# Rotary sums on VectorE instead of GpSimd, and an opening with the root ahead of the first high part and three more unread products

## The chip, the cores and the metric

The kernel runs on one core of a Trainium2 chip. That core has five engines with instruction streams of their own: TensorE (PE, matrix products into PSUM), VectorE (DVE), ScalarE (ACT), GpSimd (POOL) and SyncE (SP, which here only issues transfers). They meet through semaphores. What counts is the device time of one execution in microseconds, the median of several.

## The reference

The reference is a small decoder trunk in float32: 512 positions, width 1024, two layers. Layer 0 mixes positions by retention, layer 1 by an mLSTM; behind each stands a convolutional feed-forward block. Each block is normed by the root mean square, scaled and shifted by values computed from a conditioning vector `c`, and added to the residual. What matters here is the start of it, the retention layer's queries and keys, which get a rotary embedding:

```
def rope(t, positions):
    d = t.shape[-1]
    inv_freq = ROPE_BASE ** (-jnp.arange(0, d, 2, dtype=jnp.float32) / d)
    ang = positions.astype(jnp.float32)[..., None] * inv_freq
    cos = jnp.cos(ang)[:, :, None, :].astype(t.dtype)
    sin = jnp.sin(ang)[:, :, None, :].astype(t.dtype)
    t1, t2 = t[..., : d // 2], t[..., d // 2:]
    return jnp.concatenate([t1 * cos - t2 * sin, t1 * sin + t2 * cos], axis=-1)

def retention_mixer(h, positions, w_in, gn_g, w_out):
    ...
    proj = h @ w_in
    q, k, v, g = jnp.split(proj, [H * dk, 2 * H * dk, 2 * H * dk + H * dv], axis=-1)
    q = rope(q.reshape(Bt, S, H, dk), positions)
    k = rope(k.reshape(Bt, S, H, dk), positions) * (dk ** -0.5)
    ...
        s = jnp.einsum('bhid,bhjd->bhij', qc, kc) * decay
        intra = jnp.einsum('bhij,bhjv->bhiv', s, vc)
```

There are four heads with queries and keys of 256 and values of 512.

## The kernel before

**Products in parts.** Each float32 operand is split into a high part (`hh`, `whi`, `qkh`: a cast on ScalarE) and a low part (`hl`, `wlo`, `qkl`: what the cast left over), and a product is three matmuls: high by high, high by low, low by high. A weight's low part comes either from VectorE (`wlo<-wv,whi`) or in two steps: ScalarE writes the negated high part and a transfer issued by GpSimd adds the weight to it in memory (`wlo<-ws`, `wlo<-wa`, `wlo<-wt`). Some matrix products are formed with fewer blocks from sums of weights, so VectorE also makes sums of weight tiles (`ws<-wv,wv`, `wt<-wa,wb`). ScalarE copies one finished product to `fs`, and VectorE adds it to another (`p<-p,fs`, `pv<-pv,fs`).

**What sets the order.** Nothing is issued as it is written. Every call goes into a `Plan` (class at L153) with a modelled cost; a list scheduler (`order` L222, `run` L268) gives each engine one fixed order by due times counted from TensorE's own order, and only then are the instructions issued, nearly all of them from one line (L387). Moving one step from an engine to another therefore changes the order of its neighbours too. Once the program runs, each engine works through its own fixed list, and an instruction that waits holds up all behind it on that engine. The model charges a VectorE operation more when it runs beside a GpSimd operation with two inputs (`SHARE`, L346 to L350).

**Rotary embedding.** `rope` (L1552) takes the two halves of one head's q or k, each 128 rows by 512 positions, out of PSUM, and forms four products with `cos` and `sin` on VectorE (`rp<-p,cos`; for the first head `rp<-pp,cos`). A difference and a sum of two of these, on GpSimd, give the embedded halves (`rp<-rp,rp`), whose high parts ScalarE casts (`qkh`) and whose low parts VectorE takes (`qkl`). That is done for q and k of four heads: 16 such sums. Heads follow one another, with products of other parts in between; the sums fall between 89 and 315 us.

**The opening.** `ret_start` (L1611) reads x and sums the squares (`pms`, `means`), takes the root on ScalarE (`rc<-pms,eps_t`, L1706) and its reciprocal on VectorE, spreads it over 128 rows by four products with a unit matrix (`pms<-eye,rc`, L1714), scales x with it (`xr`, VectorE), casts (`hh`, ScalarE) and starts the products with the first weights `w_s`, whose high parts are casts (`whi<-raw`, by `high`). While TensorE has nothing to do it is given matmuls of ones whose result is never read (`pst<-warm,ones`, function `busy`, L1623). How many is set by `BUSY` and `EXTRA` (L54 and L55): `BUSY[1] + EXTRA[1]` ahead of the four products with the unit matrix (L1713), `BUSY[2] + EXTRA[2]` behind them (L1717). Those of `EXTRA` have no cost in the plan (`free`). The opening's calls carry one pin, which keeps them in the order in which they are written on each engine.

**Conditioning.** `ada<-ada,c_ext` is a VectorE operation that multiplies a 128x1025 tile of conditioning weights by `c` and sums each row; many of these are spread through the program.

Of the kernel before, what the change touches and what calls it, by code (L numbers as in the profile page):

```python
# [13 lines left out]
AF = mybir.ActivationFunctionType  # L14
ALU = mybir.AluOpType
# [36 lines left out]
HURRY = 1.5  # L52
ROPE_DUE = 200.0
BUSY = (6, 1, 1)  # L54
EXTRA = (4, 1, 3)  # L55
ALIVE = (0, 0, 256, 256, 256, 256, 0, 0)
SUMMED = 6
LOWK = 5
# [332 lines left out]
def trunk(ctx: ExitStack, tc: tile.TileContext, xT, cb, pos, vec, ident, decay, zmask, ada, w_s0, w_in0, w_v0,  # L391
# [20 lines left out]
    def slot(s, dt=F32, w=T):  # L412
        return tile_of(slots, [P, w], dt, "s", uid(s))
# [4 lines left out]
    def bank(s):  # L418
        return tile_of(psum, [P, T], F32, "ps", uid(s))
# [4 lines left out]
    def fixed(pool, shape, dt, name):  # L424
        b = tile_of(pool, shape, dt, name, name)
        b.get()
        return b

    plan = Plan()
    V, A, G, PE, S = (plan.engine(*p) for p in (("DVE", nc.vector), ("ACT", nc.scalar), ("POOL", nc.gpsimd),  # L430
                                                ("PE", nc.tensor), ("SP", nc.sync)))
# [28 lines left out]
    def col(name, i):  # L460
        return vecs[:, VEC[name] + i : VEC[name] + i + 1]

    eps_t = fixed(const, [P, 1], F32, "eps_t")
# [7 lines left out]
    def gemv(layer, f, raw):  # L471
        return V.scalar_tensor_tensor(raw, raw, 1.0, c_ext[:], op0=ALU.mult, op1=ALU.mult,
                                      accum_out=mods[layer][:, f : f + 1])
# [11 lines left out]
    def gain(layer, which, k):  # L485
        f = (8, 32)[which] + k
        i = which * KT + k
        V.tensor_scalar(gains[layer][:, i : i + 1], mods[layer][:, f : f + 1], 1.0,
                        col(("ntok", "nffn")[which], layer * KT + k), op0=ALU.add, op1=ALU.mult)


    def high_part(raw, off=0):
        hi = wide("whi", F32R)[:, off : off + raw.width]
        A.copy(hi, raw)
        return hi
# [158 lines left out]
    def pair_of(s, src):  # L654
        p = Pair(s)
        p.split(src)
        return p
# [894 lines left out]
    def rope(p1, p2):  # L1552
        t = [slot("rp")[:] for _ in range(4)]
        V.tensor_tensor(t[0], p1[:], cos[:], op=ALU.mult)
        V.tensor_tensor(t[1], p2[:], sin[:], op=ALU.mult)
        V.tensor_tensor(t[2], p1[:], sin[:], op=ALU.mult)
        V.tensor_tensor(t[3], p2[:], cos[:], op=ALU.mult)
        G.tensor_tensor(t[0], t[0], t[1], op=ALU.subtract)
        G.tensor_tensor(t[2], t[2], t[3], op=ALU.add)
        return [pair_of("qk", t[n]) for n in (0, 2)]  # L1560

    def half_pair(st, name, finish):
# [48 lines left out]
    def ret_start():  # L1611

        rs, rc = slot("rs"), slot("rc")
        warm = slot("warm", F32R)
        G.memset(warm[:].bitcast(F32), 1.0)
        pss, ps = [bank("pst") for _ in range(5)], bank("pms")
# [6 lines left out]
        def busy(n, w=T, free=0):  # L1623

            for i in range(n):
                c = PE.matmul(pss[0][:, :w], ones["1"][:], warm[:, :w], start=True, stop=True, skip_group_check=True)
                if i >= n - free:
                    c.occ = 0.0
# [9 lines left out]
        def high(k):  # L1638
            wh[k] = high_part(raw[k])
# [11 lines left out]
        def means(m, first):  # L1651

            for t in range(4):
                PE.matmul(ps[:, t : t + 1], sq[m][:, t * P : t * P + P], ones["d"][:, :1].bitcast(F32),
                          start=first and t == 0, stop=True, skip_group_check=True)
# [38 lines left out]
        for m in range(1, KT):  # L1694
# [3 lines left out]
            else:  # L1698
                busy(EXTRA[0], free=EXTRA[0])
                means(m - 1, True)  # L1700
            alive(m, ALIVE[m])
        means(KT - 1, False)
        gemv(0, KT, mod[KT])
        gain(0, 0, 0)
        high(0)
        A.activation(rc[:, :4], ps[:, :4], AF.Sqrt, bias=eps_t[:])  # L1706
        V.reciprocal(rc[:, :4], rc[:, :4])
        pin, plan.pin, plan.soon, plan.behind = plan.pin, None, ROPE_DUE, len(plan.calls) - 1
        for _ in tables:
# [2 lines left out]
        gemv(0, 0, mod[0])  # L1712
        busy(BUSY[1] + EXTRA[1], free=EXTRA[1])  # L1713
        for t in range(4):  # L1714
            PE.matmul(ps[:, t * P : t * P + P], rc[:, t : t + 1].broadcast_to([P, P]), eye[:, :P], start=True,
                      stop=True, skip_group_check=True)
        busy(BUSY[2] + EXTRA[2], free=EXTRA[2])  # L1717
        xr = xrs[0] = slot("xr")
# [45 lines left out]
    def ret_q(i, between=nothing):  # L1764
        thens = [half_pair(R[i], name, rope) for name in ("q", "k")]
        if i:
            fold_pairs(pair_srcs(w_in0, i * 8), sums0.terms, thens, between, i == 2)
            return
        for n, then in enumerate(thens):
            for j in range(2):  # L1770
                proj_item(w_in0[i * 8 + 2 * n + j], h0, then, 2 * n + j in QLOW)
        item([], lambda w: sums_early())
# [167 lines left out]


    sums0.xr.update(ret_start())
    for n, (uses, fn, free) in enumerate(items):
        gate = len(plan.calls)
# [128 lines left out]
```

## Time and profile before

| | |
|---|---|
| median of 3 runs | 1476.16 us (1475.42 to 1477.04) |
| the profiled execution's own time | 1476.27 us |
| its span | 1474.5 us |
| VectorE, of the span | 88% |
| ScalarE | 72% |
| GpSimd | 18% |
| clock granted to TensorE, mean | 0.996 |

The span runs from the first to the last recorded instruction; the execution's time is 1.8 us longer. Times in the rows of the profile count from the start of the span. In a row of the timeline stand the start, the duration, the engine and the line, the operation with the names of what it writes and reads (`out<-in`), its size, and in brackets how long the engine had stood idle before it and which instruction or transfer ended that. In a row of stretches stand the stretch, its length, the busy time of TensorE, its weight loads, VectorE, ScalarE and GpSimd with their instruction counts, the clock granted to TensorE, the share of the transfer engines and their GB/s. In a row of waits stand the total, how often, and the longest.

### The profile page before, as it was taken

To read this page: it belongs to the slowest core of one execution; us is meant where nothing else is said; L and a number is where in the kernel's file an instruction comes from. 1 tells how busy PE (TensorE), PEld (TensorE's weight loads), DVE (VectorE), ACT (ScalarE), POOL (GpSimd) and SP (SyncE) were. 2 spreads that over 40 slices of the span, in tenths; PEclk is the share of its full clock that TensorE was granted. 3 is DMA by queue.
4 is the path that set the end of the run, shared out by engine and by line. 5 is a ranking of instruction groups with operands and counts; after the bars stand their busy time and mean duration, and the time that the engine had idled before them with its cause. 6 is when DMAs were issued, how large, how long until landed. Compare 5 with 4: busy or idle time off the path is not lost. (4 is left out here: it accounts for less than half of the span.)

```text
span 1474.5 us, 27411 instructions
## 1 busy us (share of the span) xinstructions
PE 1457.1 (99%) x10561; PEld 1367.3 (93%) x10561; DVE 1291.8 (88%) x2167; ACT 1064.2 (72%) x1604; POOL 267.9 (18%) x295
## 2 busy tenths in 40 slices
PE   9999999999999999999999999999999999999998
PEld 6899999998999999999999998999989999999997
DVE  7999989787989999898897999999989988886866
ACT  5678858776588776676678985989856877667673
POOL 0334223222011111011001321222121011101010
PEclk9999999999999999999999999999999999999999
DMA  9878989887588999899467876878877678668661
GB/s 365 250 179 202 287 218 245 225 250 197 159 223 216 260 262 256 217 241 246 150 185 171 210 207 188 193 194 198 253 192 191 166 184 204 153 171 205 171 162 59
DMA packets 90822, 306.16 MB, mean 208 GB/s; under 512 B 11954, under 2 KB 14514, under 8 KB 90691
## 3 DMA queue, kind: packets, MB, share of 16 engines
q1 hardware_dynamic: 60882, 197.18, 38.8%
q0 software_dynamic: 29520, 106.97, 38.8%
q8 instruction: 82, 1.34, 0.3%
q10 hardware_dynamic: 288, 0.27, 0.1%
q14 instruction: 50, 0.40, 0.1%
HBM read 195.29 MB, written 2.12 MB: 134 GB/s over the span
## 5 line engine op out<-in xcount | busy, mean ns | idle before, releaser
L387 PE MATMUL p<-hh,whi 128*128 128x256 f32 (+1 forms) x1029 | 284.2, 277 | 2.1 <-DVE p L387 2.0
L387 PE MATMUL p<-hl,whi 128*128 128x256 f32 x1024 | 283.0, 277 | 0.0
L387 PE MATMUL p<-hh,wlo 128*128 128x256 f32 x1024 | 280.9, 277 | 0.2 <-DMA wlo<-ws 0.2
L387 ACT ACTIVATE wlo<-whi 128x1024 fp32r<-128x1024 f32 (+1 forms) x205 | 215.5, 1055 | 23.0 <-PE po L387 14.9
L387 PEld LDWEIGHTS p<-hh,whi 128*128 128x128 f32 x1029 | 193.5, 188 | 3.6 <-DVE p L387 2.9
L387 PEld LDWEIGHTS p<-hl,whi 128*128 128x128 f32 x1024 | 192.4, 188 | 0.4
L387 PEld LDWEIGHTS p<-hh,wlo 128*128 128x128 f32 x1024 | 191.3, 188 | 0.4 <-DMA wlo<-ws 0.4
L387 PE MATMUL p<-t24h,whi 128*128 128x256 f32 x768 | 169.7, 278 | 2.9 <-DVE p L387 1.9
L387 PE MATMUL po<-ggl,whi 128*128 128x512 f32 (+1 forms) x448 | 152.4, 342 | 0.0
L387 PE MATMUL po<-ggh,wlo 128*128 128x512 f32 (+1 forms) x448 | 151.9, 342 | 0.0
L387 PE MATMUL po<-ggh,whi 128*128 128x512 f32 (+1 forms) x448 | 151.3, 343 | 0.0
L387 PE MATMUL p<-t24l,whi 128*128 128x256 f32 x512 | 141.8, 277 | 0.0
L387 DVE SCALAR_TENSOR_TENSOR x<-po,mod,x 128x512 f32<-128x512 f32 (+1 forms) x184 | 113.4, 628 | 29.8 <-PE po L387 28.9
L387 ACT CAST whi<-raw 128x1024 fp32r<-128x1024 f32 (+1 forms) x113 | 113.8, 1017 | 35.4 <-DMA raw<-w_s 12.2
L387 PEld LDWEIGHTS p<-t24h,whi 128*128 128x128 f32 x768 | 130.2, 188 | 5.2 <-DVE p L387 2.3
L387 DVE SCALAR_TENSOR_TENSOR cv<-p,vecs,cv 128x511 f32<-128x511 f32 (+1 forms) x152 | 111.2, 743 | 12.0 <-ACT cv L387 11.7
L387 DVE SCALAR_TENSOR_TENSOR ada<-ada,c_ext 128x1025 f32<-128x1025 f32 x96 | 119.7, 1248 | 0.6 <-DMA ada<-ada 0.6
L387 PE MATMUL po<-yl,whi 128*128 128x256 f32 (+1 forms) x352 | 115.3, 328 | 0.0
L387 PE MATMUL po<-yh,whi 128*128 128x256 f32 (+1 forms) x354 | 115.2, 327 | 0.0
L387 PE MATMUL po<-yh,wlo 128*128 128x256 f32 (+1 forms) x352 | 115.2, 327 | 0.0
L387 POOL DMA_DIRECT2D wlo<-wa x55 | 47.6, 866 | 350.5 <-ACT wlo L387 168.8
L387 ACT CAST whi<-ws 128x1024 fp32r<-128x1024 f32 x88 | 92.0, 1049 | 21.7 <-DVE ws L387 15.0
(292 smaller groups left out, 4419.1 us busy)
## 6 DMA issues: line engine op xcount, KB each, us to landing
ada<-ada SPq DMA_DIRECT2D x96, 512.5 KB, 7.0
wlo<-ws POOLq DMA_DIRECT2D x61, 512.0 KB, 6.9
wlo<-wa POOLq DMA_DIRECT2D x55, 512.0 KB, 6.3
wlo<-wt POOLq DMA_DIRECT2D x45, 512.0 KB, 6.6
wa<-w_up SPq DMA_DIRECT2D x38, 512.0 KB, 5.8
wb<-w_up SPq DMA_DIRECT2D x38, 512.0 KB, 7.0
wlo<-raw POOLq DMA_DIRECT2D x34, 512.0 KB, 8.0
raw<-w_o SPq DMA_DIRECT2D x32, 512.0 KB, 8.0
```

Of the source, the lines that this page charges most:

```text
L387: getattr(c.obj, c.name)(*[real(v) for v in c.a], **{key: real(v) for key, v in c.k.items()})
```

## The change

Three edits:

- the 16 rotary sums go from GpSimd (`G`) to VectorE (`V`)
- the root of the opening is written ahead of the first high part
- `EXTRA` is (4, 2, 5): one unread matmul more ahead of the products with the unit matrix, two more behind them

```diff
-EXTRA = (4, 1, 3)
+EXTRA = (4, 2, 5)
...
         V.tensor_tensor(t[2], p1[:], sin[:], op=ALU.mult)
         V.tensor_tensor(t[3], p2[:], cos[:], op=ALU.mult)
-        G.tensor_tensor(t[0], t[0], t[1], op=ALU.subtract)
-        G.tensor_tensor(t[2], t[2], t[3], op=ALU.add)
+        V.tensor_tensor(t[0], t[0], t[1], op=ALU.subtract)
+        V.tensor_tensor(t[2], t[2], t[3], op=ALU.add)
         return [pair_of("qk", t[n]) for n in (0, 2)]
...
         gain(0, 0, 0)
+        A.activation(rc[:, :4], ps[:, :4], AF.Sqrt, bias=eps_t[:])
         high(0)
-        A.activation(rc[:, :4], ps[:, :4], AF.Sqrt, bias=eps_t[:])
         V.reciprocal(rc[:, :4], rc[:, :4])
```

The plan is made anew from these calls. The orders of the engines differ in the opening and then between about 60 and 330 us; behind that they are the same. Three places follow.

VectorE around the second head's rotary products, some 105 to 120 us into the program; `rp` are rotary tiles, `ws` sums of weights, `sl` the low part of weighted scores. Before:

```order
L387 TENSOR_TENSOR p_186_875<-p_186_875,fs_879 128x256
L387 TENSOR_TENSOR sl_1064<-sp_1084,sh_1051 128x256
L387 TENSOR_TENSOR sl_1064<-sp_1084,sh_1051 128x128
L387 TENSOR_TENSOR p_224_970<-p_223_988,fs_1002 128x256
L387 TENSOR_TENSOR rp_1163<-p_186_875,cos_798 128x512
L387 TENSOR_TENSOR rp_1174<-p_186_875,sin_784 128x512
L387 TENSOR_TENSOR ws_1181<-ws_1124,wv_891 128x1024
L387 TENSOR_TENSOR ws_1196<-wv_891,wv_894 128x1024
L387 TENSOR_TENSOR wlo_1217<-wv_1027,whi_1169 128x1024
L387 TENSOR_TENSOR ws_1230<-wv_1027,ws_1181 128x1024
L387 TENSOR_TENSOR rp_1247<-p_224_970,sin_784 128x512
L387 TENSOR_TENSOR rp_1253<-p_224_970,cos_798 128x512
```

and now:

```order
L387 TENSOR_TENSOR rp_1164<-p_186_878,cos_821 128x512
L387 TENSOR_TENSOR rp_1171<-p_186_878,sin_798 128x512
L387 TENSOR_TENSOR ws_1180<-ws_1136,wv_856 128x1024
L387 TENSOR_TENSOR p_224_956<-p_223_1029,fs_1035 128x256
L387 TENSOR_TENSOR sl_1074<-sp_1133,sh_1068 128x128
L387 TENSOR_TENSOR ws_1200<-wv_856,wv_894 128x1024
L387 TENSOR_TENSOR wlo_1215<-wv_1013,whi_1129 128x1024
L387 TENSOR_TENSOR ws_1232<-wv_1013,ws_1180 128x1024
L387 TENSOR_TENSOR rp_1250<-p_224_956,sin_798 128x512
L387 TENSOR_TENSOR rp_1259<-p_224_956,cos_821 128x512
L387 TENSOR_TENSOR rp_1164<-rp_1164,rp_1089 128x512
L387 TENSOR_TENSOR rp_1171<-rp_1171,rp_1113 128x512
```

The second `ws` now stands ahead of one `p` and one `sl` step, and the head's first two sums (the last two rows) come eight rows behind it. The first head's four sums stand further ahead.

VectorE at a later head's products, some 207 to 216 us into the program. Before:

```order
L387 TENSOR_TENSOR ws_2342<-wv_2144,wv_2182 128x1024
L387 TENSOR_TENSOR p_416_2191<-p_416_2191,fs_2197 128x256
L387 TENSOR_TENSOR rp_2365<-p_416_2191,cos_798 128x512
L387 TENSOR_TENSOR rp_2374<-p_416_2191,sin_784 128x512
L387 TENSOR_TENSOR wlo_2400<-wv_2243,whi_2379 128x1024
L387 TENSOR_TENSOR p_439_2260<-p_438_2306,fs_2310 128x256
L387 TENSOR_TENSOR ws_2424<-wv_2243,ws_2299 128x1024
```

and now:

```order
L387 TENSOR_TENSOR ws_2347<-wv_2143,wv_2184 128x1024
L387 TENSOR_TENSOR rp_2363<-p_417_2170,cos_821 128x512
L387 TENSOR_TENSOR p_416_2192<-p_416_2192,fs_2197 128x256
L387 TENSOR_TENSOR rp_2379<-p_416_2192,cos_821 128x512
L387 TENSOR_TENSOR p_439_2261<-p_438_2309,fs_2313 128x256
L387 TENSOR_TENSOR ws_2397<-wv_2244,ws_2320 128x1024
L387 TENSOR_TENSOR wlo_2412<-wv_2244,whi_2390 128x1024
```

The step on `p_439` stood behind the low part `wlo`, and now stands two rows ahead of it.

TensorE in the opening, with the unread matmuls as `pst<-warm,ones`. Before:

```order
L387 MATMUL pms_211<-ones_d,sq_194 128x1 x4
L387 MATMUL pms_211<-ones_d,sq_200 128x1 x4
L387 MATMUL pst_117<-warm_97,ones_81 128x512 x2
L387 MATMUL pms_211<-eye_134,rc_110 128x128 x4
L387 MATMUL pst_117<-warm_97,ones_81 128x512 x4
```

and now:

```order
L387 MATMUL pms_211<-ones_d,sq_194 128x1 x4
L387 MATMUL pms_211<-ones_d,sq_200 128x1 x4
L387 MATMUL pst_117<-warm_97,ones_81 128x512 x3
L387 MATMUL pms_211<-eye_134,rc_110 128x128 x4
L387 MATMUL pst_117<-warm_97,ones_81 128x512 x6
```

Two became three and four became six; on ScalarE the root `rc` and the cast `whi` behind it have changed places, and the rows that follow them, the second cast and then the two `hh`, are as before.

## The prediction

> **What bounds the kernel now.** I read the page's busy shares first, then TensorE's waits over the part of the program in which the change moves anything (the first 340 us), then the stretches in which those waits fall.
>
> ```profile
> PE 1457.1 (99%) x10561; PEld 1367.3 (93%) x10561; DVE 1291.8 (88%) x2167; ACT 1064.2 (72%) x1604; POOL 267.9 (18%) x295
> ```
> ```profile
> PE p L387 <- DVE p L387: 1.6, 1, 1.6
> PE pv L387 <- ACT fs L387: 1.4, 1, 1.4
> ```
> ```profile
> 120.00:125.00 5.00, 3.60 (x31) 3.40 (x30) 5.00 (x6) 5.00 (x10) 4.28 (x4) 1.00 1.05 200
> 210.00:215.00 5.00, 3.36 (x28) 3.16 (x27) 4.72 (x3) 4.16 (x8) 3.88 (x4) 1.00 1.08 194
> ```
> TensorE is busy for 99% of the span, so a change that leaves its matmuls alone can only win back gaps. The two longest waits of this part fall into the two stretches shown: there TensorE works 3.60 and 3.36 of 5 us, while VectorE is busy for nearly all of it. The gaps themselves, in TensorE's timeline (start, duration, and in brackets what it waited for):
>
> ```profile
> 121.16 0.28 PE L387 MATMUL pv<-wlo,hh 128*128 128x256 f32 x1
> 121.28 0.28 PE L387 MATMUL pv<-whi,hl 128*128 128x256 f32 x1
> 122.95 0.39 PE L387 MATMUL pv<-whi,hh 128*128 128x256 f32 x1 [1.40 <-ACT fs L387]
> 126.29 0.38 PE L387 MATMUL pv<-whi,t24h 128*128 128x256 f32 x1 [0.24 <-DVE pv L387]
> 214.49 0.39 PE L387 MATMUL p<-t24h,whi 128*128 128x256 f32 x1 [1.64 <-DVE p L387]
> 319.15 0.38 PE L387 MATMUL p<-t24h,whi 128*128 128x256 f32 x1 [1.05 <-ACT fs L387]
> ```
> Undisturbed matmuls start 0.12 us apart (121.16 to 121.28). The one at 122.95 starts 1.67 after its predecessor, so 1.55 are lost there, 0.15 more than the bracket says. Adding that 0.15 to the other brackets gives losses of 0.4 (126.29), 1.8 (214.49) and 1.2 (319.15). I call them **gaps 1 to 4**.
>
> What is late ahead of each? ScalarE's, VectorE's and GpSimd's timelines:
>
> ```profile
> 115.18 1.06 ACT L387 CAST whi<-ws 128x1024 fp32r<-128x1024 f32 x1 [3.90 <-DVE ws L387]
> 122.54 0.36 ACT L387 COPY fs<-pv 128x256 f32<-128x256 f32 x1
> ```
> ```profile
> 94.50 1.77 DVE L387 TENSOR_TENSOR wt<-wa,ws 128x512 f32<-128x512 f32 x1
> 110.95 4.19 DVE L387 TENSOR_TENSOR ws<-ws,wv 128x1024 f32<-128x1024 f32 x1
> 115.07 1.21 DVE L387 TENSOR_TENSOR ws<-wv,wv 128x1024 f32<-128x1024 f32 x1
> 125.81 0.42 DVE L387 TENSOR_TENSOR pv<-pv,fs 128x256 f32<-128x256 f32 x1
> 210.28 3.82 DVE L387 TENSOR_TENSOR wlo<-wv,whi 128x1024 fp32r<-128x1024 f32 x1 [0.74 <-ACT whi L387]
> 214.02 0.42 DVE L387 TENSOR_TENSOR p<-p,fs 128x256 f32<-128x256 f32 x1
> ```
> ```profile
> 111.20 2.85 POOL L387 TENSOR_TENSOR rp<-rp,rp 128x512 f32<-128x512 f32 x2
> 209.21 1.62 POOL L387 TENSOR_TENSOR rp<-rp,rp 128x512 f32<-128x512 f32 x1
> 211.07 1.93 POOL L387 TENSOR_TENSOR rp<-rp,rp 128x512 f32<-128x512 f32 x1
> ```
> The same 128x1024 sum takes 1.21 us at 115.07 and 4.19 at 110.95, where two of GpSimd's rotary sums run beside it; 4.19 less 1.21 is 2.98, about the 2.85 that the two sums last. The split at 210.28 takes 3.82 beside two more. Gap 1: `ws` ends at 115.14, ScalarE has idled 3.90 for it and from 115.18 is busy without a break, so the copy `fs` starts only at 122.54 and TensorE waits. Gap 3: `p<-p,fs` stands behind the 3.82 and starts at 214.02; TensorE follows at 214.49. Gap 2 has the same cause through the `ada` product ahead of 125.81, the longest of this row:
>
> ```profile
> L387 DVE SCALAR_TENSOR_TENSOR ada<-ada,c_ext x96: 1165/1221/2778, 13.6 to 1189.0; 128x1025 f32<-128x1025 f32 x96
> L387 POOL TENSOR_TENSOR rp<-rp,rp x16: 1263/1618/2136, 89.1 to 313.1; 128x512 f32<-128x512 f32 x16
> ```
>
> **The change part by part.** *The sums.* GpSimd loses 16 instructions of 1.62 us (median), 26 us of an engine that is 18% busy: nothing by itself. VectorE gains 16 of the same shape as its products:
>
> ```profile
> 87.71 0.68 DVE L387 TENSOR_TENSOR rp<-pp,cos 128x512 f32<-128x512 f32 x1
> 88.31 0.68 DVE L387 TENSOR_TENSOR rp<-pp,sin 128x512 f32<-128x512 f32 x1
> ```
> They start 0.60 apart, so the sums cost 16 x 0.60 = 9.6 us. Two bounds: 0.60 if they follow like these, 0.68 if a sum must wait for its whole product (10.9 in all). I take 0.60, as a sum's product mostly stands two or more rows ahead of it. What goes: 2.98 (`ws`), 3.82 less 1.21 = 2.61 (`wlo`), 2.78 less 1.22 = 1.56 (`ada`) and 1.77 less about 0.68 = 1.09 (`wt`, at 94.50), 8.2 in four rows. VectorE's load is thus about level; what counts is where it falls.
>
> The Trainium skill ("VectorE: DVE Perf Modes", section "The DRAIN you can't avoid") says that a VectorE operation does not start until the one before it has emptied the pipe, which speaks for the dearer price, 10.9. The rows above start 0.08 before their predecessor's end, so the trace bears out 0.60; by the page six sums would take 0.5 off the margin at gap 2 below, and the sum would stay.
>
> Up to gap 1: in the new order four sums (2.4) stand ahead of that `ws`, while a `sl` and a `p` step (together 0.6) move behind it; 1.1 of `wt` goes. It would start at 110.95 + 2.4 - 0.6 - 1.1, or 111.65, less up to 0.7 that VectorE idled on the way (I count none of it), and with 1.2 instead of 4.19 end at 112.9, 2.3 earlier than 115.14. Gap 1 needs ScalarE 1.55 earlier, so **gap 1 closes** (-1.55; bounds -1.0, were the sums dearer and the idling kept, and -1.55). Up to gap 2: six sums (3.6) against 2.98 + 1.56 + 1.1 gone and two `qkl` (1.2) moved behind: `pv` could come 3.2 earlier than 125.81. With gap 1 closed TensorE is there 1.55 earlier, and wants it 0.4 earlier still, 1.95 in all: **gap 2 closes** (-0.4, bounds 0 and -0.4), with 1.3 to spare.
>
> Gap 3: no GpSimd sum is left beside the split, and `p` now stands ahead of it on VectorE; the sums of that head come behind. **Gap 3 closes** (-1.8; bounds 0, if the `fs` that feeds it is what comes next, and -1.8).
>
> Gap 4 stays. VectorE there does two low parts ahead of the step that TensorE needs:
>
> ```profile
> 317.15 1.49 DVE L387 TENSOR_TENSOR qkl<-rp,qkh 128x512 fp32r<-128x512 f32 x2
> ```
> They end at 318.64, `fs` follows them; the order of these rows is unchanged, but on ScalarE a `whi` cast (1.06 in the row at 115.18) now stands ahead of `fs`. It fits beside the two low parts except for a piece: +0.2, bounds 0 and +1.06.
>
> *The opening.* ScalarE, then TensorE:
>
> ```profile
> 15.00 1.05 ACT L387 CAST whi<-raw 128x1024 fp32r<-128x1024 f32 x1 [3.50 <-DMA raw<-w_s]
> 15.95 0.26 ACT L387 ACTIVATE rc<-pms,eps_t 128x4 f32<-128x4 f32 x1
> 18.80 1.04 ACT L387 CAST whi<-raw 128x1024 fp32r<-128x1024 f32 x1 [2.59 <-DMA raw<-w_s]
> 19.75 0.91 ACT L387 ACTIVATE hh<-xr,mod 128x256 fp32r<-128x256 f32 x2
> ```
> ```profile
> 16.48 2.08 PE L387 MATMUL pms<-eye,rc 128*128 128x128 f32 x8 [0.84 <-DVE rc L387]
> 18.20 2.05 PE L387 MATMUL pst<-warm,ones 128*128 128x512 f32 x4
> 20.31 2.08 PE L387 MATMUL pst<-whi,hh 128*128 128x512 f32 x4
> ```
> The root no longer waits for the cast, which brings it, the reciprocal and the `eye` products forward by up to 0.95 (15.95 less 15.00). But the first real product at 20.31 needs `hh` (19.75), and `hh` stands on ScalarE behind the second cast, which idles 2.59 for a transfer and starts at 18.80. That order is unchanged, so the early root has nothing to give. The unread matmuls cost up to 0.5 each here (2.05 for four): the one ahead of `eye` fits into the 0.84 in which TensorE waited, and the two behind add 1.0 to a row that the earlier `eye` starts 0.85 sooner. They end about 0.2 later than now, by 20.4 against 20.31: at most +0.2. And that is taken back later:
>
> ```profile
> 47.04 1.05 ACT L387 CAST whi<-raw 128x1024 fp32r<-128x1024 f32 x1 [2.43 <-DMA raw<-w_in]
> 48.76 1.20 PE L387 MATMUL pst<-whi,hh 128*128 128x512 f32 x4
> ```
> ScalarE idles again for a transfer until 47.04, and the `hh` behind that cast is what the product at 48.76 needs. Whatever TensorE gains or loses by 47 us is levelled there: 0, bounds -0.3 and +0.2.
>
> **The sum:** -1.55 - 0.4 - 1.8 + 0.2 + 0 = -3.55. The profiled execution took 1476.27 us (span 1474.5 and 1.8 around it), 0.11 over the median of the runs, so the sum stands for that too: 1472.7.
>
> **The rivals.** *A transfer caps gaps 1 and 2.* GpSimd's row, the transfers issued around it (KB, median us to landing), and TensorE's product that reads the tile:
>
> ```profile
> 141.48 0.90 POOL L387 DMA_DIRECT2D wlo<-wa  x1 [0.95 <-ACT wlo L387]
> wlo<-wa POOLq DMA_DIRECT2D x1, 512.0 KB, 9.6
> 151.38 0.28 PE L387 MATMUL p<-hh,wlo 128*128 128x256 f32 x1
> ```
> 141.48 + 9.6 is 151.1, so that landing is 0.3 ahead of its reader. If it does not come earlier, the 1.95 of gaps 1 and 2 shrink to 0.3 and the sum to -0.3 - 1.8 + 0.2 = -1.9: 1474.4. For it: transfers depend on one another's queue. Against it: this one was issued when ScalarE had its source ready, and ScalarE comes earlier.
>
> *The opening comes through.* Four products take 2.08 at 20.31 and 1.20 at 48.76, 0.9 less for the four, because the clock granted around 20 us is half:
>
> ```profile
> 15.83:19.24 3.41, 2.77 (x11) 2.57 (x12) 2.96 (x7) 0.82 (x3) 0.00 (x0) 0.50 1.03 418
> ```
> If a denser row of unread matmuls brings the full clock at the end of this stretch, those four products are 0.9 faster; if the transfers before 47.04 come earlier too, that is kept: 1471.8. The 2.59 and 2.43 of idling for transfers speak against it.
>
> The Trainium skill ("TensorE: Matmul & The Clock Gate", section "Part 1: The HAM clock gate") has the full clock granted after one busy window of about 3.4 us, the windows running freely. The stretch above, of 3.41 at half clock with TensorE busy for 2.77 of it, does not contradict that; by that rule the earlier grant is likely, though not that the end gains by it.
>
> *Nothing reaches the end*: other late steps take the gaps' place within a few tenths, 1476.
>
> *Slower.* GpSimd's sums are not what holds VectorE up (its transfers' issues, say, are), and VectorE gets the sums on top. Six of them (3.6) lie ahead of gap 2; with 0.6 and 1.2 moved behind, gaps 1 and 2 grow by 1.8; at gap 3 two sums more are 1.2: 1479.3. It decides once less than 1.8 of the 4.5 at `ws` and `ada` goes. Against it stands that the 2.98 match the 2.85 of the two sums.
>
> **How the numbers follow.** Forecast 0.45, the capping transfer 0.23, the opening 0.07, nothing 0.11, slower 0.14. The forecast's own range is 1471.8 to 1473.6 by the bounds of gap 1 and gap 4. About 0.2% (2.95 us, to 1473.2) is what a measurement of this kernel can tell from no change. Faster: 0.36 of the forecast, the opening, 0.04 of the cap: 0.47. Slower: most of the last case and a little of "nothing", 0.14. Same: 0.39. The range goes from 1471.0, below the opening case by what gap 4 could give, to 1477.6, the lower end of the slower case (bounds of its 3.0: 1.8 at gaps 1 and 2 alone, less 0.4), and leaves out some 0.15.
>
> **What would show it.** VectorE's `ws` and `wlo` at 1.2 us where they took 4.19 and 3.82; ScalarE's idle of 3.90 ahead of `whi` gone or shorter; no TensorE wait for `fs` near 121 nor for `p` near 212; a wait of about 1 us for `fs` near 315; the product after 20 us no earlier, and TensorE level with before at 49. A TensorE wait for `wlo` near 149 would show the cap; `qkl` or `psc` waits near 102 would show VectorE short.

## The result and the profile after

| | before | changed |
|---|---|---|
| median of 22 runs each | 1476.83 us | 1474.92 us |
| ratio, 95% interval | | 0.9984 (0.9976 to 0.9992) |
| profiled execution's span | 1474.5 us (first), 1475.2 us (second) | 1474.7 us (first), 1471.6 us (second), 1476.5 us (third) |

The changed kernel is faster by 0.16%, with an interval of 0.08% to 0.24%, or 1.2 to 3.5 us. Now and then an execution runs at a lower granted clock: one of the 22 of the changed kernel took 1905.26 us at 0.713 and is left out of the ratio, and one of the twelve of "moved3_opening" below took 1493.43 us at 0.946 and is left in, which widens that run's interval. Two later measurements of the changed kernel, beside runs of the kernel before, gave 0.9976 (0.9965 to 0.9987) and 0.9976 (0.9964 to 0.9988). The forecast of 3.55 us less is 0.24%: the end of the first interval, the middle of the other two. The first measurement found about two thirds of it.

The first profile of the changed kernel is of an execution that took 1476.48 us, above the median, and its span is no shorter than before. It has to be read by stages, then. First the page's busy times, which answer to the first line shown before:

```profile
PE 1458.4 (99%) x10564; PEld 1370.7 (93%) x10564; DVE 1289.8 (87%) x2183; ACT 1063.3 (72%) x1604; POOL 244.5 (17%) x279
```

VectorE has 16 instructions more and 2.0 us less busy time (1291.8 to 1289.8); GpSimd has 16 fewer and 23 us less. The two stretches in which the longest gaps lay:

```profile
120.00:125.00 5.00, 5.00 (x45) 5.00 (x44) 3.51 (x8) 4.72 (x9) 0.85 (x1) 1.00 1.06 264
210.00:215.00 5.00, 5.00 (x47) 5.00 (x46) 5.00 (x8) 4.08 (x7) 0.86 (x1) 1.00 1.05 179
```

TensorE works 5.00 of 5 us in both, where it worked 3.60 and 3.36. VectorE's rows behind it:

```profile
111.69 1.21 DVE L387 TENSOR_TENSOR ws<-ws,wv 128x1024 f32<-128x1024 f32 x1
119.92 1.22 DVE L387 SCALAR_TENSOR_TENSOR ada<-ada,c_ext 128x1025 f32<-128x1025 f32 x1
123.84 0.43 DVE L387 TENSOR_TENSOR pv<-pv,fs 128x256 f32<-128x256 f32 x1 [1.49 <-PE pv L387]
210.62 1.22 DVE L387 TENSOR_TENSOR wlo<-wv,whi 128x1024 fp32r<-128x1024 f32 x1
```

The sum that took 4.19, the `ada` product that took 2.78 and the low part that took 3.82 all take 1.2. At `pv` it is now VectorE that waits for TensorE, 1.49 us. ScalarE, which had idled 3.90 for the sum of weights and then started `fs` at 122.54:

```profile
113.11 1.05 ACT L387 CAST whi<-ws 128x1024 fp32r<-128x1024 f32 x1
120.94 0.37 ACT L387 COPY fs<-pv 128x256 f32<-128x256 f32 x1 [0.20 <-PE pv L387]
```

The cast starts 2.07 earlier, at 113.11 for 115.18, and `fs` now waits for TensorE. What TensorE still waits for between 60 and 340 us, first profile and then second:

```profile
PE p L387 <- ACT fs L387: 2.1, 2, 1.1
PE pv L387 <- DMA wlo<-ws: 0.5, 1, 0.5
```
```profile
PE p L387 <- ACT fs L387: 1.0, 1, 1.0
PE pv L387 <- DMA wlo<-ws: 0.5, 1, 0.5
```

The waits for VectorE's `p` (1.6) and for `fs` at `pv` (1.4) are gone. One for `fs` near 316 us stays. Two are new: one for a transfer, in both profiles, and one more for `fs`, in the first only. In TensorE's timeline of the first profile:

```profile
90.48 0.39 PE L387 MATMUL p<-t24h,whi 128*128 128x256 f32 x1 [1.06 <-ACT fs L387]
223.46 0.39 PE L387 MATMUL pv<-wlo,t3h 128*128 128x256 f32 x1 [0.49 <-DMA wlo<-ws]
316.92 0.39 PE L387 MATMUL p<-t24h,whi 128*128 128x256 f32 x1 [1.07 <-ACT fs L387]
```

The last of these is the matmul that started at 319.15 before. It starts 2.23 us earlier in the first profile; in the second, at 316.42, 2.73 earlier. In a third profile, taken later, it starts at 317.71, 1.44 earlier. That lead is what the change does up to here; much of what comes behind it differs between executions.

### The profile page after: what moved, and what is told of

It reads as the page before. It is cut to its first block, busy times and chain, and to the rows that moved or that the text cites. A ratio compares the mean times of both kernels' runs of the same rounds, so it can differ in the third digit from the quotient of the medians.

```text
span 1474.7 us, 27429 instructions
## 1 busy us (share of the span) xinstructions
PE 1458.4 (99%) x10564; PEld 1370.7 (93%) x10564; DVE 1289.8 (87%) x2183; ACT 1063.3 (72%) x1604; POOL 244.5 (17%) x279
## 4 chain that ended last, share of the span: by engine, by line
PE 49%; DMA 1%; ACT 1%; DVE 1%; issue 1%; DVEq 0%; POOL 0%; POOLq 0%
PE p L387 20%; PE po L387 16%; PE pv L387 5%; PE pf L387 3%; PE pav L387 2%; DMA wlo<-wt 1%; PE psc L387 1%; ACT whi L387 0%; PE pp L387 0%; ACT mc L387 0%; DVE sl L387 0%; DVE mc L387 0%; ACT wlo L387 0%; ACT L387 0%; DVE ws L387 0%
```

## The experiments

Three theories were held against each other. A: GpSimd's sums hold VectorE up, and moving them is the gain. B: the opening brings it. C: it is the new order of the plan that counts, not the engine of the sums. Each time is the median beside runs of the kernel before on the same chip; the ratio is worked out from the runs and is not the quotient of the two medians. "Moved_opening" has 5 runs, "moved3" 7, the others 9 to 12.

| run | us | before | ratio (95%) |
|---|---|---|---|
| sums alone | 1476.06 | 1478.42 | 0.9986 (0.9976 to 0.9996) |
| opening alone | 1477.17 | 1478.42 | 0.9997 (0.9987 to 1.0006) |
| moved | 1474.81 | 1478.42 | 0.9977 (0.9968 to 0.9985) |
| held | 1482.07 | 1478.42 | 1.0023 (1.0013 to 1.0032) |
| again | 1474.49 | 1478.31 | 0.9976 (0.9965 to 0.9987) |
| moved3 | 1474.04 | 1478.31 | 0.9971 (0.9959 to 0.9982) |
| moved_opening | 1473.50 | 1478.31 | 0.9963 (0.9950 to 0.9975) |
| moved3_opening | 1473.68 | 1478.55 | 0.9983 (0.9959 to 1.0007) |
| again2 | 1475.02 | 1478.55 | 0.9976 (0.9964 to 0.9988) |

**The sums alone.** The kernel before with

```diff
-        G.tensor_tensor(t[0], t[0], t[1], op=ALU.subtract)
-        G.tensor_tensor(t[2], t[2], t[3], op=ALU.add)
+        V.tensor_tensor(t[0], t[0], t[1], op=ALU.subtract)
+        V.tensor_tensor(t[2], t[2], t[3], op=ALU.add)
```

> The 16 rotary sums on VectorE alone, the opening as before. Theory A (GpSimd's sums held VectorE up): the waits near 121, 126 and 212 us are gone, as in the changed kernel, and the whole of its gain is here: 1.5 to 3 us faster than before. Theory B (the denser opening brings the gain): no more than 0.5 us faster.

It is 0.14% faster, and its only waits between 60 and 340 us are 1.0 for `fs` and 0.7 for a transfer. The gain is there without the opening, so B falls. Whether it is the whole gain of the change the intervals don't tell (0.9986 against 0.9984 and 0.9976).

**The opening alone.** The kernel before with the other two edits:

```diff
-EXTRA = (4, 1, 3)
+EXTRA = (4, 2, 5)
...
+        A.activation(rc[:, :4], ps[:, :4], AF.Sqrt, bias=eps_t[:])
         high(0)
-        A.activation(rc[:, :4], ps[:, :4], AF.Sqrt, bias=eps_t[:])
```

> The early root and the three more unread matmuls alone, the sums on GpSimd. Theory A: TensorE may be up to 0.6 us ahead at 60 us, and the end is within 0.7 us of before; the waits near 121 and 212 us stay. Theory B: 1.5 us faster or more.

Within its interval, which reaches from 1.9 us faster to 0.9 slower, it makes no difference. TensorE's rows of the opening, and one of ScalarE's, show why, and that one step of the prediction was too simple:

```profile
15.85 1.14 PE L387 MATMUL pms<-eye,rc 128*128 128x128 f32 x8
16.74 1.63 PE L387 MATMUL pst<-warm,ones 128*128 128x512 f32 x6
20.24 1.20 PE L387 MATMUL pst<-whi,hh 128*128 128x512 f32 x4 [1.86 <-ACT hh L387]
48.10 1.20 PE L387 MATMUL pst<-whi,hh 128*128 128x512 f32 x4 [0.16 <-ACT hh L387]
```

```profile
46.37 1.05 ACT L387 CAST whi<-raw 128x1024 fp32r<-128x1024 f32 x1 [2.71 <-DMA raw<-w_in]
```

The products with the unit matrix start 0.63 earlier, and in this execution the clock stayed at full (granted 1.00 from 12 to 24 us; six unread matmuls in 1.63, where four took 2.05). TensorE then waits 1.86 for `hh`, so the first real product moves from 20.31 to 20.24 only. The one at 48.76 comes at 48.10, as the cast that it depends on (the last row, ScalarE's) has its transfer at 46.37 instead of 47.04. The lead at 48 us is 0.66. At gap 4's matmul, at 318.84, it is 0.31 against the first profile of before and 0.72 against the second; at the end no gain can be told.

The changed kernel has the same opening, but in its first profile the granted clock was 0.50 from 16 to 20 us:

```profile
18.36 2.91 PE L387 MATMUL pst<-warm,ones 128*128 128x512 f32 x6
21.06 1.16 PE L387 MATMUL pst<-whi,hh 128*128 128x512 f32 x4
```

There the six unread matmuls last until the first real product, which starts 0.75 later than before. In the second profile the clock was 0.62 in that stretch and the product starts at 20.30; in the second profile of the kernel before, with the old opening, 0.57 and 20.40. So when the full clock comes differs between executions, and these traces don't show that the added matmuls bring it.

**Moved: the old order, the new engine.** The plan is made as before, with the sums counted on GpSimd, and only the engine that gets them is exchanged:

```diff
-        G.tensor_tensor(t[0], t[0], t[1], op=ALU.subtract)
-        G.tensor_tensor(t[2], t[2], t[3], op=ALU.add)
+        G.tensor_tensor(t[0], t[0], t[1], op=ALU.subtract).obj = nc.vector
+        G.tensor_tensor(t[2], t[2], t[3], op=ALU.add).obj = nc.vector
```

> The plan of before, kept row for row on every engine, except that the 16 sums are issued on VectorE at the place in the program where GpSimd had them. Theory A: the sum of weights near 111 us and the low part near 210 us take 1.2 us instead of 4.2 and 3.8, the waits near 121 and 212 us go, and as ScalarE's order is that of before, the new wait of 1.1 us near 89 us is not there: 2.5 to 4 us faster than before. Theory C (the gain comes from the new order, the place of the sums counts for nothing): within 0.7 us of before, or slower by the 9.6 us of added VectorE work as far as that shows.

It is 0.23% faster, with every other row in its old place, so the new order is not needed for the gain. The two rows that took 4.19 and 3.82, now without GpSimd's sums beside them:

```profile
111.79 1.22 DVE L387 TENSOR_TENSOR ws<-ws,wv 128x1024 f32<-128x1024 f32 x1
209.47 1.22 DVE L387 TENSOR_TENSOR wlo<-wv,whi 128x1024 fp32r<-128x1024 f32 x1
```

The waits near 121, 126 and 212 are gone. One wait was not expected:

```profile
92.47 0.39 PE L387 MATMUL p<-hh,whi 128*128 128x256 f32 x1 [1.28 <-DVE p L387]
```

On VectorE two of the first head's sums now stand ahead of the `p` step that it needs (starts: 89.00 and 91.40 the sums, 92.00 `p`, which was at 91.04):

```profile
89.00 0.67 DVE L387 TENSOR_TENSOR rp<-rp,rp 128x512 f32<-128x512 f32 x1
91.40 0.67 DVE L387 TENSOR_TENSOR rp<-rp,rp 128x512 f32<-128x512 f32 x1
92.00 0.41 DVE L387 TENSOR_TENSOR p<-p,fs 128x256 f32<-128x256 f32 x1
```

**Held: the new order, the old engine.** The opposite exchange in the changed kernel:

```diff
-        V.tensor_tensor(t[0], t[0], t[1], op=ALU.subtract)
-        V.tensor_tensor(t[2], t[2], t[3], op=ALU.add)
+        V.tensor_tensor(t[0], t[0], t[1], op=ALU.subtract).obj = nc.gpsimd
+        V.tensor_tensor(t[2], t[2], t[3], op=ALU.add).obj = nc.gpsimd
```

> The plan of the changed kernel, kept row for row, except that the 16 sums are issued on GpSimd at the place where VectorE had them. Theory A: some VectorE operations with two operands in SBUF take 2.5 to 4 us again, waits near 110 to 130 and 210 us return, 1 to 4 us slower than the changed kernel. Theory C: as fast as the changed kernel.

It is slower than the kernel before, 1482.07 for 1478.42, and by the ratios some 6 to 7 us slower than the changed kernel, more than the 1 to 4 expected. Nor do the waits stand where they were expected: the `ws` near 113 and the `wlo` near 213 take 1.2, as the sums now fall beside other rows. Its longest waits between 60 and 340 us are near 322, 104 and 247:

```profile
PE p L387 <- ACT fs L387: 2.3, 1, 2.3
PE psc L387 <- DVE qkl L387: 0.9, 1, 0.9
PE p L387 <- DMA wlo<-wa: 0.8, 1, 0.8
```

One of VectorE's slow rows, and GpSimd's beside it:

```profile
221.12 3.62 DVE L387 TENSOR_TENSOR wlo<-wv,whi 128x1024 fp32r<-128x1024 f32 x1
```
```profile
220.81 2.84 POOL L387 TENSOR_TENSOR rp<-rp,rp 128x512 f32<-128x512 f32 x2
```

A low part of the size that takes 1.2 alone takes 3.62, the difference of 2.4 close to the 2.5 for which the two sums run beside it (221.12 to 223.65). The issue of a transfer on GpSimd has no such effect:

```profile
113.29 1.21 DVE L387 TENSOR_TENSOR ws<-ws,wv 128x1024 f32<-128x1024 f32 x1
```
```profile
113.38 0.87 POOL L387 DMA_DIRECT2D wlo<-ws  x1 [9.31 <-DVE rp L387]
```

With the same order on both sides, the engine of the 16 sums is worth some 5 to 7 us here (1.0023 against 0.9986 with the sums alone, and against 0.9976 with the opening too). C falls. Of A, "moved" shows the half that matters most: the same rows in the same order are fast without the sums beside them. "Held" shows what the engine costs in the new order, but not all of that is VectorE being held up. The sums themselves are done later: near 315 ScalarE waits 0.76 for one, ahead of the casts that the wait of 2.3 near 322 hangs on. How the 5 to 7 us divide was not worked out.

**A second profile of both kernels.**

> The changed kernel once more, for a second profile. Where its first profile lost what it had gained (1.7 us between 700 and 790 us, where matmuls started 0.118 us apart instead of 0.113, and 0.8 us near 645): if that belongs to the change, it is there again; if it varies from one execution to the next, these places look different, and only the first 360 us are alike, 2 to 3 us ahead of before. Time: 1.2 to 3.5 us faster than before, as measured already.

> The kernel before once more, for a second profile: the waits near 121, 126, 212 and 318 us are there again, within 0.2 us. Behind 360 us stretches with matmuls 0.118 us apart may stand in other places, with 1 to 2 us of difference between the two profiles of one kernel.

In the second profile of the kernel before, the four waits are there again within 0.1 us (1.4, 0.2, 1.6 and 1.0). One stretch of each profile shows a place where the first profile of the change lost some of its lead. The numbers with an x are counts of instructions in 20 us, the first of them of TensorE's matmuls, in the order before, before again, changed, changed again:

```profile
720.00:740.00 20.00, 20.00 (x179) 20.00 (x178) 16.91 (x38) 13.68 (x24) 2.61 (x3) 1.00 0.50 143
```
```profile
720.00:740.00 20.00, 20.00 (x172) 20.00 (x171) 16.20 (x37) 13.42 (x24) 2.57 (x3) 1.00 0.49 142
```
```profile
720.00:740.00 20.00, 20.00 (x173) 20.00 (x172) 16.20 (x38) 14.63 (x25) 2.60 (x3) 1.00 0.56 155
```
```profile
720.00:740.00 20.00, 20.00 (x179) 20.00 (x178) 16.91 (x40) 16.97 (x31) 2.61 (x3) 1.00 0.60 168
```

In one profile of each kernel TensorE gets through 179 matmuls, in the other through 172 or 173, at a granted clock of 1.00 and busy for all of the 20 us. That is 0.7 to 0.8 us lost in 20 us, and it happens to the kernel before as well: it belongs to the execution, not to the change. The wait near 89 us is absent from the second profile, the one near 222 us is there again.

The other loss, near 643 us, is there again too: TensorE waits 0.72 and 0.86 for a cast `whi` of a weight, and 0.86 in "sums alone". Neither profile of the kernel before has that wait. The third profile of the change has a wait of 1.08 for such a cast at 495 us instead. Other waits are shorter in turn: between 340 and 1460 us the waits of 0.15 and more add up to 2.4, 3.4 and 2.6 in the three profiles of the change, and to 3.3 and 2.5 in the two of before. So on the whole the change neither gains nor loses by waits behind gap 4.

**Moved3: the first head stays on GpSimd.** As "moved", but

```diff
+        sums = [G.tensor_tensor(t[0], t[0], t[1], op=ALU.subtract), G.tensor_tensor(t[2], t[2], t[3], op=ALU.add)]
+        for c in sums if len(roped) > 2 else ():
+            c.obj = nc.vector
```

where `roped` counts the calls of `rope`, two for each head.

> As the run with the plan of before and the sums issued on VectorE, but the first head's four sums stay on GpSimd. There the wait for VectorE at 91 us was 1.45 us instead of 0.3, with two sums ahead of the step that TensorE needed. Theory A: that wait is back at 0.3, the waits near 121, 126 and 212 us stay away, and it is 0.5 to 1.5 us faster than that run, some 4 to 5 us faster than before. Rival (added VectorE work has slack, the 1.45 is made good later by transfers): the same time as that run.

The wait near 91 us is gone from the list of waits, and those near 121, 126 and 212 stay away. The time, 0.29% below before, is 0.06% below that of "moved": the intervals overlap, so the trace shows the step and the times neither confirm nor exclude it. The matmul of gap 4 starts at 315.83, where "moved" has it at 316.36.

**Moved with the opening.**

> The plan of before with all 16 sums issued on VectorE, and the opening of the change. If the opening gives nothing, as its run alone suggests: within 0.7 us of the run without it, 2.5 to 4 us faster than before. If it gives what TensorE has gained at 60 us: 0.6 us faster than that run.

0.9963 is the lowest ratio of all, but its interval meets those of "moved" and of "again". Whether the opening gives something in this order was not settled.

**All together, beside the changed kernel.**

> The plan of before with the first head's sums left on GpSimd, the other twelve issued on VectorE, and the opening of the change. By the traces so far it has none of the waits near 91 (beyond 0.3), 121, 126, 212 and 222 us; what stays is the one near 315. If waits removed add up: 0.7 us faster than the changed kernel (the wait near 222) to 1.5 us, 4 to 5 us faster than before. Rival: later stretches level such differences, and it is within 0.5 us of the changed kernel on the same chip.

> The changed kernel beside it on the same chip, with a third profile: 2 to 4 us faster than before; the waits near 222 and 315 us are there again, that near 89 us of the first profile is not.

The medians, 1473.68 and 1475.02, differ by 1.3 us, more than the removed wait alone, but the interval of the first (0.9959 to 1.0007) is too wide to tell them apart. Its longest run aside, its runs still lie between 1471.38 and 1477.03, and those of the changed kernel between 1471.89 and 1478.24. In its profile gap 4's matmul starts at 315.49, 3.66 earlier than before and 0.9 to 2.2 earlier than in the three profiles of the change, and the waits near 91, 121, 126, 212 and 222 are absent, as expected. The third profile of the change did have the wait near 89 us, against what was expected.

## Why the prediction came out as it did

- **What holds VectorE up**: right. The slow rows lay beside GpSimd's sums, "moved" makes the same rows fast in the same order, and "held" brings such rows back in another. The rival, that the issues of transfers hold VectorE up, falls with the `ws` at 113.29 in "held".
- **Gaps 1 and 2** (-1.95): right, with the margin roughly as worked out. `pv` had 1.49 to spare where 1.3 was worked out. ScalarE's cast came 2.07 earlier where 2.3 was.
- **Gap 3** (-1.8): right, the wait is absent from all profiles with the sums on VectorE.
- **Gap 4** (+0.2): it stayed, with 1.07 and 0.98 on its bracket against 1.05, so the term is 0. The forecast's own range, 1471.8 to 1473.6, does not follow from the bounds that it names: with gap 1 at -1.0 to -1.55 and gap 4 at 0 to +1.06 it is 1472.5 to 1474.1.
- **The price of the sums** (0.60 each): right. In the changed kernel's VectorE timeline a sum starts 0.60 behind the row in front of it, and the next row 0.60 behind the sum:

```profile
92.71 0.68 DVE L387 TENSOR_TENSOR rp<-pp,cos 128x512 f32<-128x512 f32 x1
93.31 0.68 DVE L387 TENSOR_TENSOR rp<-rp,rp 128x512 f32<-128x512 f32 x1
93.91 0.68 DVE L387 TENSOR_TENSOR rp<-pp,sin 128x512 f32<-128x512 f32 x1
```

- **VectorE's load**: it was put at about level, 9.6 more against 8.2 less, and fell by 2.0. Four rows that were not counted had been slow beside the sums as well: the `qkl` at 121.80 and 221.67, the `ws` at 292.09 and the `ada` at 298.21 (1.38, 1.41, 1.46 and 1.72 for 0.68, 0.68, 0.68 and 1.22).
- **The terms that were missing**: a wait for a transfer, the `wlo` near 222 us, 0.49 to 0.7 on its bracket and thus some 0.7 of time with the 0.15 added. The prediction weighed such a cap at 151 us, where none appeared, so the median's nearness to the 1474.4 of that case is chance. "Moved", whose TensorE order is the old one, has no such wait, and "held", with the new order, has one of 0.16: that speaks for the new order as what brings it. So -1.95 - 1.8 + 0.7 is -3.05, against a lead of 2.23, 2.73 and 1.44 us at gap 4's matmul in three profiles. Most of the rest is in the next point.
- **"Whatever TensorE gains or loses by 47 us is levelled there"**: wrong, as the transfer ahead of that product itself came 0.67 earlier with the opening alone. In three profiles of the change the product that started at 48.76 starts at 48.35, 49.15 and 48.36: 0.41 ahead, 0.39 behind and 0.40 ahead, outside the bounds of -0.3 and +0.2 each time. That the median of the opening alone shows no gain is therefore no proof of the reason given. In the changed kernel an early TensorE meets something that the prediction did not look at, between 56 and 90 us. VectorE works without a pause from about 58 to 95 us, and what it feeds at 89 us has no slack. In the first profile of the change `fs` starts at 90.06, and TensorE waits 1.06 for it at 90.48:

```profile
90.06 0.37 ACT L387 COPY fs<-p 128x256 f32<-128x256 f32 x1
```

In the second, `fs` starts at 89.69, and TensorE's matmul, which comes to that point later, finds it done. VectorE's row from which the stretch runs on, in before, in the first profile of the change and in the second:

```profile
55.98 1.23 DVE L387 TENSOR_TENSOR wlo<-raw,whi 128x1024 fp32r<-128x1024 f32 x1 [0.21 <-ACT whi L387]
```
```profile
56.72 1.22 DVE L387 TENSOR_TENSOR wlo<-raw,whi 128x1024 fp32r<-128x1024 f32 x1 [2.45 <-ACT whi L387]
```
```profile
56.37 1.23 DVE L387 TENSOR_TENSOR wlo<-raw,whi 128x1024 fp32r<-128x1024 f32 x1 [0.21 <-ACT whi L387]
```

From that row to `fs` it is 32.9 us in before (`fs` at 88.90) and 33.3 in both profiles of the change, so the new order costs 0.4 here. In the first profile the row comes 0.35 later than in the second besides, as the cast ahead of it had waited 2.44 for a transfer, and TensorE is 0.80 earlier. The third profile is like the first (`fs` at 90.05, a wait of 1.04), "sums alone" like the second (product at 48.79, no wait). These starts agree with that account; a run that shifts the opening alone by a set time was not made.

With the start at 48 us and the waits taken in, each with 0.15 added, the lead at gap 4 comes out: 0.41 + 3.75 - 1.21 - 0.64 is 2.3 for the first profile, where 2.23 was measured, and -0.39 + 3.75 - 0.68 is 2.7 for the second, where 2.73 was. For the third, which also waits 0.17 for a transfer at 243 us, 0.40 + 3.75 - 1.19 - 0.82 - 0.32 is 1.8, where 1.44 was; 0.4 is also what the two profiles of the kernel before differ by at that matmul (319.15 and 319.56).

So the mechanism was right and the three gaps closed as forecast, but the forecast stood too high. It left out 0.7 at 222 us and, in some executions, 1.2 at 89 us; the leads of 1.4 to 2.7 us at gap 4 agree with the 1.2 to 3.5 of the first measurement. That the later measurements meet 3.55 all the same is in part luck: the three medians of the changed kernel lie between 1474.49 and 1475.02, while those of the kernel before moved from 1476.83 to 1478.55.

## What to carry to other kernels

Work on an engine that is 18% busy is not free if operations of the busy one take longer beside it: look at the longest duration of each shape, not at its mean, and at what runs beside it. Before a change to a planned kernel is judged, exchange only the engine and keep the order, and then only the order: here the engine alone gained 0.23%, the new order with the old engine (and the new opening) lost 0.23%, and with the new engine the two orders can't be told apart (0.9977 and 0.9976). With gains of 0.2%, compare the start of one and the same matmul in two profiles of each kernel, since the end of a single one says as much about that execution as about the change.

## What the runs showed of the hardware

Several VectorE operations with two operands in SBUF were held for about as long as GpSimd's two-operand sums ran: 4.19, 3.82 and 3.62 us in place of 1.2, beside 2.85, two of 1.62 and 1.93, and 2.84 us of sums. Those that read PSUM showed no such delay: four rotary products with PSUM inputs beside GpSimd's first sums, at 89.24 to 92.0 in the kernel before, keep their 0.68 us.

```profile
89.24 0.68 DVE L387 TENSOR_TENSOR rp<-pp,cos 128x512 f32<-128x512 f32 x1
90.44 0.68 DVE L387 TENSOR_TENSOR whi<-wb,whi 128x512 fp32r<-128x512 f32 x1
91.37 0.68 DVE L387 TENSOR_TENSOR rp<-pp,sin 128x512 f32<-128x512 f32 x1
```
```profile
89.08 3.19 POOL L387 TENSOR_TENSOR rp<-rp,rp 128x512 f32<-128x512 f32 x2
```

Some rows speak against a simple rule: `whi<-wb,whi` at 90.44 reads two operands in SBUF and is not held either, nor is a `ws<-wv,ws` at 290.62 (1.22), beside a sum from 290.86 that itself takes 2.14. Both start before the sum that they then run beside (the second of the two above starts at 90.60), but so did the row of 4.19 at 110.95, with its sums from 111.20. Why was not settled.

And TensorE has two paces at the same granted clock: 179 or 172 matmuls between 720 and 740 us at 1.00, each in one profile of each kernel. What sets the pace was not tried.
